# A two-layer decoder trunk on one Trainium2 core: a chained block pair makes its weight sum in place of a loaded tile, a fourth pair in the first FFN, and the mLSTM's output gate chained to its value pair

## The chip, the cores and the metric

The kernel runs on one core of one Trainium2 chip. The metric is the device time of one launch in microseconds (us). Before the change it is 1004.13 us, the median of 3 runs (1003.7 to 1004.54). A difference under 0.2%, about 2.0 us, can hardly be told from no change. The engines are named as the profile names them: PE is TensorE (matrix products), DVE is VectorE, ACT is ScalarE, POOL is GpSimd, SP is SyncE, which here only issues DMAs.

## The reference, cut to what matters

The input x is 256 tokens by 1024 features, f32. Two layers follow one another; each layer adds four sub-layers to x, and two of the four are FFNs:

```
def swiglu(x, w_in, w_out):
    gate, up = jnp.split(x @ w_in, 2, axis=-1)      # w_in 1024 x 5632
    return (jax.nn.silu(gate) * up) @ w_out         # w_out 2816 x 1024
...
h = swiglu(rms_norm(x, g[0]), w_ffn_in[layer, 0], w_ffn_out[layer, 0])
x = x + 0.5 * rms_norm(h, g[1])
h = rms_norm(x, g[2])
    # layer 0: mLSTM mixer, layer 1: differential attention
x = x + rms_norm(h, g[3])
h = swiglu(rms_norm(x, g[4]), w_ffn_in[layer, 1], w_ffn_out[layer, 1])
x = x + 0.5 * rms_norm(h, g[5])
gate = jax.nn.sigmoid(rms_norm(x, g[6]) @ w_ple_gate[layer])
x = x + rms_norm((p[layer] @ w_ple_proj[layer]) * gate, g[7])
```

The mLSTM mixer multiplies its input by one wide matrix, whose parts are the queries, keys, values (1024 columns) and the output gate o (1024 columns); its result is `(sigmoid(o) * h) @ w_out`. After layer 0 a shared K and V is made from x for the attention of layer 1. So there are four FFNs, called here FFN(0,0), FFN(0,1), FFN(1,0) and FFN(1,1) by layer and place.

## The kernel before, in words

**Tiles.** The 256 tokens are two tiles of 128 (t = 0 and 1). The 2816 hidden columns of an FFN are 11 blocks of 256 (`NJ`). A block's input weights are the 256 gate and the 256 up columns for 1024 features, 2 MB, which are loaded as two tiles of 1 MB, one for each half of the features. Such a tile is 128 partitions by 2048 f32 numbers and is called `wraw`. There are `NRAW` = 10 buffers of this kind; the attention and the mLSTM, the parameters of the norms and x itself lie in the same buffers.

**f32 products from three.** TensorE multiplies in a reduced f32 format here. So each operand is split in two parts, hi and lo, and a product is the sum of hi·hi, lo·hi and hi·lo (`mm3`, line 507). For a weight tile ACT writes the hi part (`whi`, 6 buffers, `NPART`) and DVE subtracts it from the tile for the lo part (`wlo`, 5 buffers, `NLOW`). A tile that is added or loaded therefore costs one pass of ACT and one of DVE over 2048 numbers. A product of a 128-token tile with half the features by one block is 12 matmuls of 128x512 (`times`).

**Pairs.** The function `block_pair` (line 718) takes two blocks of weights at a time. Two blocks, two token tiles and two feature halves are a 2x2 by 2x2 block product, and it is done with 7 products instead of 8, by sums of tokens (`forms`: s1, s2, s3, n4) and sums of weights. With b11 and b21 the two halves of the first block, b12 and b22 those of the second, the weight operands are: w11, w21 and w22 (tiles as loaded); t3 = b12 + b22 and u1 = b11 + b12 (made by a load and a second DMA on POOL's queue that adds into the loaded tile, an accumulate DMA); wt2 = b11 + t3 and wt4 = b21 + b11 (added by DVE). So a pair loads 5 tiles on SP's queue (b12 for t3, b11 for u1, b11, b21, b22) and accumulates 2 on POOL's. It keeps four products as copies that ACT takes out of the accumulator (`held`, rows `att<-accI`), and DVE adds or subtracts them. `PAIRS` (line 44) lists the first blocks of the pairs: 5, 7 and 9 in FFN(0,0), and 1, 3, 5, 7 and 9 in each other FFN. The blocks that are in no pair are done by 8 products a two of them. A pair that follows another one finds its t3 and u1 loaded already: the pair ahead of it issues these two loads with their accumulates (`nxt`, `ahead`). A pair of this kind is called chained here. The order of the products in a pair is w11, w21 (then `use(0, 0)`, the SwiGLU of block 0 and token tile 0), wt2, wu1, wt3, w22, wt4 (in the last pair of an FFN w22 stands ahead of wt3). Once a pair's seven products are recorded, the kernel records the output products of the blocks before it (`stage_out`, accumulators `accO`).

**mLSTM.** The value columns and the output-gate columns are two calls of `block_pair` (lines 1082 and 1170), each with all its own loads.

**The order of the work.** All operations are first recorded. A planner, `Notes.play` (line 290), then replays them on a model of the engines and queues: on each engine it takes, among what can start now, urgent work first and then the lowest rank, and it hands the buffers out in turn. `Notes.issue` (line 433) emits the result. So every instruction has line 433 in the profile, and groups are told apart by the names of the tiles. The names that matter: `wraw` a weight tile, `whi` and `wlo` its parts, `xh` and `xl` those of the tokens, `accI` the accumulators of the input products, `accO` those of the output products, `att` a held copy, `hh` and `hl` the parts of the hidden values, `sg` the SwiGLU.

The weight operands of a pair, in the order in which they are recorded before the change:

```
t3, u1 = ahead or (load(src2[0], src2[1]), load(src[0], src2[0]))
b11 = load(src[0])
w11 = parts(b11)
b21 = load(src[1])
w21 = parts(b21)
wt2 = add(b11, b11, t3)
wu1 = parts(u1)
wt3 = parts(t3)
b22 = load(src2[1])
w22 = parts(b22)
ahead = (load(nxt[1][0], nxt[1][1]), load(nxt[0][0], nxt[1][0])) if nxt else None
wt4 = add(b21, b21, b11)
```

## Time and profile before

| what | value |
|---|---|
| median of 3 runs | 1004.13 us (1003.7 to 1004.54) |
| the profiled execution: its own time | 1002.59 us |
| the profiled execution: its span | 1000.8 us |
| granted clock of TensorE, mean | 0.997 |
| PE busy | 986.4 us, 99% |
| DVE busy | 892.8 us, 89% |
| ACT busy | 698.6 us, 70% |
| moved by the DMA engines | 274.68 MB, mean 274 GB/s |

The span is the time from the first to the last record of the profile; 1.8 us of the execution's own time lie outside it. The profiled execution is 1.54 us quicker than the median. By the matmuls that read hidden values (`hh`), the FFNs lie in the span thus: FFN(0,0) from the start to about 190 us, FFN(0,1) from about 300 to 470, FFN(1,0) to about 720 (most of it from 575 on), FFN(1,1) from about 830 to about 970. Busy time of PE is from the start of a matmul to its modelled end, and matmuls overlap; a better measure of what a matmul costs is the distance between the starts of two in a row.

### The profile page before, as it was taken

The numbers are of one execution on the slowest core, as the hardware profiler recorded it, in microseconds if no ns is written. First come the engines' busy times: TensorE is split into PE (matmuls) and PEld (weight loads), VectorE is DVE, ScalarE is ACT, GpSimd is POOL, SyncE is SP. The second block draws the span as 40 slices with busy tenths as digits, with TensorE's granted clock in tenths as the row PEclk, the third lists the DMA queues.
The fourth block names the chain that finished last, engine by engine and source line by source line (L and its number), as shares of the span: only waits on it lengthen the run. The fifth ranks groups of instructions, "written<-read, shape, count | busy, mean of one in ns | idle before, by whom it ended". The sixth has DMA issues, their size and how long they took to land.

```text
span 1000.8 us, 12442 instructions
## 1 busy us (share of the span) xinstructions
PE 986.4 (99%) x4636; PEld 803.0 (80%) x4636; DVE 892.8 (89%) x909; ACT 698.6 (70%) x924; POOL 94.9 (9%) x126
## 2 busy tenths in 40 slices
PE   9999999999999999999999999999999999999997
PEld 7888888887787778888878888888888887878786
DVE  6977999799999999998799999898984999999983
ACT  7746777578756877685867767686776776757752
POOL 0010000300141000001120000001002300000010
PEclk9999999999999999999999999999999999999998
DMA  9999948765699999765699999864759899996621
GB/s 345 420 339 343 311 179 296 244 207 198 255 320 340 326 309 335 279 247 207 261 301 330 324 353 347 329 244 161 253 210 285 235 297 318 313 295 252 242 84 43
DMA packets 45859, 274.68 MB, mean 274 GB/s; under 512 B 5480, under 2 KB 5864, under 8 KB 16104
## 3 DMA queue, kind: packets, MB, share of 16 engines
q1 hardware_dynamic: 39752, 231.69, 60.2%
q0 software_dynamic: 5760, 41.95, 20.6%
q8 instruction: 36, 0.59, 0.2%
q10 hardware_dynamic: 288, 0.27, 0.1%
q14 instruction: 23, 0.19, 0.1%
HBM read 263.40 MB, written 10.49 MB: 274 GB/s over the span
## 4 chain that ended last, share of the span: by engine, by line
PE 47%; issue 2%; ACT 2%; POOL 1%; DVE 1%; DVEq 0%; POOLq 0%; ACTq 0%
PE accI L433 30%; PE accO L433 15%; PE tr L433 2%; POOL sm L433 1%; ACT sg L433 1%; DVE wlo_4r L433 0%; ACT att L433 0%; DVE wlo_2r L433 0%; ACT wraw L433 0%; ACT whi_5r L433 0%; ACT whi_0r L433 0%; DVE wraw L433 0%; DVE att L433 0%; DVE xl_5r L433 0%; DVEq L1498 0%
## 5 line engine op out<-in xcount | busy, mean ns | idle before, releaser
L433 DVE TENSOR_TENSOR wraw<-wraw,wraw 128x2048 f32<-128x2048 f32 x40 | 91.4, 2284 | 0.1
L433 ACT ACTIVATE whi_1r<-wraw 128x2048 fp32r<-128x2048 f32 (+2 forms) x49 | 72.7, 1494 | 18.2 <-PE accI L433 8.8
L433 ACT ACTIVATE whi_4r<-wraw 128x2048 fp32r<-128x2048 f32 (+1 forms) x45 | 75.4, 1684 | 11.9 <-issue 4.4
L433 ACT ACTIVATE whi_2r<-wraw 128x2048 fp32r<-128x2048 f32 (+1 forms) x48 | 79.4, 1661 | 5.5 <-issue 2.6
L433 ACT ACTIVATE whi_5r<-wraw 128x2048 fp32r<-128x2048 f32 (+1 forms) x47 | 79.2, 1694 | 5.6 <-PE accI L433 4.7
L433 ACT ACTIVATE whi_0r<-wraw 128x2048 fp32r<-128x2048 f32 (+2 forms) x48 | 74.5, 1557 | 6.8 <-PE accI L433 3.4
L433 ACT ACTIVATE whi_3r<-wraw 128x2048 fp32r<-128x2048 f32 (+1 forms) x45 | 73.6, 1647 | 3.3 <-PE accI L433 1.6
L433 ACT ACTIVATE att<-accI 128x512 f32<-128x512 f32 x80 | 47.5, 594 | 38.1 <-PE accI L433 37.8
L433 POOL DMA_DIRECT2D wraw<-in_ffn_in x36 | 32.0, 889 | 343.5 <-DMA wraw<-in_ffn_in 286.3
L433 POOL TENSOR_SCALAR sm<-sm 128x1 f32<-128x1 f32 x32 | 23.5, 735 | 308.8 <-ACT sg L433 308.8
L433 POOL TENSOR_TENSOR sm<-sm,mhalf 128x1 f32<-128x1 f32 (+2 forms) x40 | 30.7, 769 | 108.2 <-DVE sm L433 105.6
L433 ACT ACTIVATE sg<-att,sm 128x256 f32<-128x256 f32 x54 | 26.9, 502 | 16.9 <-DVE att L433 16.8
L433 ACT ACTIVATE sg<-accO 128x512 bf16<-128x512 f32 (+2 forms) x46 | 20.2, 445 | 25.0 <-PE accO L433 21.0
L433 ACT ACTIVATE sg<-accI,sm 128x256 f32<-128x256 f32 x34 | 16.0, 470 | 29.3 <-PE accI L433 27.3
L433 PEld LDWEIGHTS tr<-ident,sg 128*128 128x128 f32 x176 | 23.0, 140 | 14.6 <-DVE hl_2r L433 2.7
L433 PE MATMUL tr<-ident,sg 128*128 128x128 f32 x176 | 34.0, 274 | 0.3 <-DVE hl_2r L433 0.3
L433 DVE SCALAR_TENSOR_TENSOR wraw<-wraw,sm,wraw 128x512 f32<-128x512 f32 x32 | 22.7, 749 | 12.0 <-POOL sm L433 11.9
L433 DVE TENSOR_TENSOR att<-accI,att 128x512 f32<-128x512 f32 x40 | 27.4, 685 | 3.3 <-PE accI L433 2.9
L433 ACT ACTIVATE sg<-wraw 128x512 bf16<-128x512 f32 x32 | 20.1, 630 | 13.7 <-DVE wraw L433 9.7
L433 ACT ACTIVATE att<-accI,sm 128x512 f32<-128x512 f32 (+1 forms) x22 | 14.8, 671 | 20.8 <-PE accI L433 20.8
L433 DVE SCALAR_TENSOR_TENSOR sg<-att,sm,sg 128x256 f32<-128x256 f32 x54 | 25.7, 480 | 1.7 <-ACT sg L433 1.5
L433 DVE TENSOR_TENSOR att<-att,att 128x512 f32<-128x512 f32 (+1 forms) x33 | 22.4, 679 | 3.8 <-ACT att L433 3.6
(610 smaller groups left out, 3249.9 us busy)
## 6 DMA issues: line engine op xcount, KB each, us to landing
wraw<-in_ffn_in SPq DMA_DIRECT2D x102, 1024.0 KB, 9.4
wraw<-in_ffn_out SPq DMA_DIRECT2D x44, 1024.0 KB, 8.3
wraw<-in_ffn_in POOLq DMA_DIRECT2D x36, 1024.0 KB, 13.3
wraw<-in_mlstm_in SPq DMA_DIRECT2D x14, 1024.0 KB, 5.3
wraw<-in_ple_gate SPq DMA_DIRECT2D x8, 1024.0 KB, 5.1
wraw<-in_w_kv SPq DMA_DIRECT2D x8, 1024.0 KB, 4.8
home<-wraw SPq DMA_DIRECT2D x28, 256.0 KB, 5.1
wraw<-home SPq DMA_DIRECT2D x14, 512.0 KB, 5.4
```

What stands on the lines that cost most here:

```text
L433: getattr(getattr(self.nc, eng), name)(*args, **kw)
```

## The change

- `PAIRS`: FFN(0,0) has the pairs 3, 5, 7 and 9 (before: 5, 7 and 9). Blocks 3 and 4 were done by 8 products and are now done by 7.
- A chained pair has a new order of loads and products. Its second half-block b22 is loaded into a tile and split as w22; then b12 is accumulated onto the same tile by POOL's queue, so that it becomes t3. Before, t3 was a tile of its own, loaded by the pair ahead, and b22 a further load. The pair ahead now loads u1 alone. The order of the products is wu1, w22, w11, w21 (then `use(0, 0)`), then the output products of the pair ahead (`between`), then wt2, wt3 and wt4. Five products are held as copies instead of four.
- A pair that is the first of its chain keeps the order of before.
- The mLSTM's output gate is chained to its value pair: the value pair loads the gate's u1.
- `NRAW` goes from 10 to 9, `NLOW` from 5 to 6.

There are 3 chained pairs in FFN(0,0), 4 in each other FFN and 1 in the mLSTM, 16 in all. The numbers of instructions go from before to after as follows: 128x512 matmuls 4502 to 4490; loads of `in_ffn_in` tiles of 128x2048 on SP's queue 102 to 88, and of `in_mlstm_in` 14 to 13; accumulates on POOL's queue 40 to 42; DVE's splits of whole weight tiles 190 to 193, its adds of two weight tiles 40 to 42, its adds and subtracts of held copies and forms 72 to 75; ACT's copies out of `accI` into `att` 80 to 100.

The diff, cut to its core:

```
-NRAW = 10
+NRAW = 9
-NLOW = 5
+NLOW = 6
-PAIRS = ((5, 7, 9),) + ((1, 3, 5, 7, 9),) * 3
+PAIRS = ((3, 5, 7, 9),) + ((1, 3, 5, 7, 9),) * 3
...
+        if ahead is not None:
+            nc.is_urgent = False
+            u1 = ahead
+            t3 = load(src2[1])
+            nc.is_urgent = True
+            w22 = parts(t3)
+            nc.gpsimd.dma_start(t3, src2[0], accum_op=ALU.add)
+            nc.is_urgent = False
+            wu1 = parts(u1)
+            b11 = load(src[0])
+            w11 = parts(b11)
+            b21 = load(src[1])
+            w21 = parts(b21)
+            nc.is_urgent = True
+            s1, s2, s3, n4 = xf() if callable(xf) else xf
+            az = acc_in()
+            times(az, s1, wu1, False)
+            z5 = held(az)
+            times(az, n4, w22, True)
+            z4 = held(az)
+            ax, ay = acc_in(), acc_in()
+            times(ax, quarter(0, 0), w11, False)
+            p1 = held(ax)
+            times(ay, quarter(0, 4), w21, False)
+            nc.vector.tensor_tensor(p1, ay, p1, op=ALU.add)
+            use(0, 0, p1)
+            if between:
+                between()
+            nc.is_urgent = False
+            wt2 = add(b11, b11, t3)
+            ahead = load(nxt[0][0], nxt[1][0]) if nxt else None
+            wt3 = parts(t3)
+            wt4 = add(b21, b21, b11)
+            nc.is_urgent = True
+            times(ax, s2, wt2, True)
+            u2 = held(ax)
+            nc.vector.tensor_tensor(u2, z4, u2, op=ALU.subtract)
+            use(1, 0, u2)
+            times(ax, s3, wt3, True)
...
+            use(1, 1, z5)
+            times(ax, quarter(1, 4), wt4, True)
+            use(0, 1, ax)
+            return ahead
-        t3, u1 = ahead or (load(src2[0], src2[1]), load(src[0], src2[0]))
+        t3, u1 = load(src2[0], src2[1]), load(src[0], src2[0])
...
-        ahead = (load(nxt[1][0], nxt[1][1]), load(nxt[0][0], nxt[1][0])) if nxt else None
+        ahead = load(nxt[0][0], nxt[1][0]) if nxt else None
...
+            behind = [(i, t) for t in range(NT) for i in last]
             if len(item) == 2:
                 nxt = items[begin + n + 1]
+                between = late if split_begin and n == 0 else (lambda: outs(behind)) if ahead is not None else None
...
-        block_pair(xts, all_forms(), a["mlstm_in"][2], a["mlstm_in"][3], value)
+        gates = a["mlstm_in"][4:6]
+        ahead = block_pair(xts, all_forms(), a["mlstm_in"][2], a["mlstm_in"][3], value, nxt=gates)
...
-        block_pair(xts, all_forms(), a["mlstm_in"][4], a["mlstm_in"][5], opened)
+        block_pair(xts, all_forms(), *gates, opened, ahead=ahead)
```

What moves is shown at three places. The first is POOL's queue in FFN(0,0), where the accumulates stand with the semaphores that each waits for (`DMAHW` a load, `DVE` a split or add of VectorE). Before:

```order
L433 DMA wraw_83<-in_ffn_in 128x2048 [waits DMAHW7_49]
L433 DMA wraw_84<-in_ffn_in 128x2048 [waits DMAHW0_49]
L433 DMA wraw_79<-in_ffn_in 128x2048 [waits DMAHW5_49,DMAHW6_49,DMAHW4_49,DVE_49]
L433 DMA wraw_80<-in_ffn_in 128x2048 [waits DMAHW5_49]
L433 DMA wraw_84<-in_ffn_in 128x2048 [waits DMAHW3_49]
L433 DMA wraw_83<-in_ffn_in 128x2048 [waits DMAHW4_49]
```

After:

```order
L433 DMA wraw_79<-in_ffn_in 128x2048 [waits DMAHW3_49,DMAHW1_49,DMAHW4_49,DMAHW0_49,DVE_49]
L433 DMA wraw_80<-in_ffn_in 128x2048 [waits DMAHW5_49,DMAHW6_49,DMAHW1_49,DVE_49]
L433 DMA wraw_84<-in_ffn_in 128x2048 [waits DMAHW7_49]
L433 DMA wraw_78<-in_ffn_in 128x2048 [waits DMAHW1_49,DVE_49]
L433 DMA wraw_81<-in_ffn_in 128x2048 [waits DMAHW6_49]
L433 DMA wraw_85<-in_ffn_in 128x2048 [waits DMAHW7_49,DVE_49,Activation_49]
L433 DMA wraw_78<-in_ffn_in 128x2048 [waits DMAHW4_49]
L433 DMA wraw_81<-in_ffn_in 128x2048 [waits DMAHW0_49,DVE_49]
```

Two accumulates have come in ahead for the pair of blocks 3 and 4, and the accumulate of a chained pair's t3 (here `wraw_78`, the fourth) now waits for DVE, which splits the same tile as w22 first.

The second place is DVE at the start of FFN(1,1): the end of the attention's sum and the first pair's weights. `wlo` rows are splits, `wraw<-wraw,wraw` is a weight sum, and the last row is the residual add of token tile 1, from which the FFN's second token tile starts. Before:

```order
L433 TENSOR_TENSOR wlo_2r<-wraw_79,whi_4r 128x1024
L433 TENSOR_TENSOR wlo_3r<-wraw_76,whi_0r 128x1024 x2
L433 TENSOR_TENSOR wlo_1r<-wraw_78,whi_3r 128x2048
L433 TENSOR_TENSOR wraw_80<-accO_93,wraw_80 128x512
L433 TENSOR_TENSOR wraw_80<-accO_95,wraw_80 128x512
L433 TENSOR_TENSOR wlo_4r<-wraw_83,whi_5r 128x2048
L433 TENSOR_TENSOR wraw_78<-wraw_78,wraw_85 128x2048
L433 SCALAR_TENSOR_TENSOR sg_126<-accI_90,sm_6_162,sg_126 128x256
L433 SCALAR_TENSOR_TENSOR wraw_77<-wraw_80,sm_7_163,wraw_77 128x512 x2
```

After:

```order
L433 TENSOR_TENSOR wlo_3r<-wraw_82,whi_5r 128x1024
L433 TENSOR_TENSOR wlo_5r<-wraw_81,whi_0r 128x2048
L433 TENSOR_TENSOR wlo_1r<-wraw_85,whi_4r 128x2048
L433 TENSOR_TENSOR wraw_79<-accO_93,wraw_79 128x512
L433 TENSOR_TENSOR wraw_79<-accO_96,wraw_79 128x512
L433 TENSOR_TENSOR wraw_81<-wraw_81,wraw_83 128x2048
L433 TENSOR_TENSOR wraw_85<-wraw_85,wraw_81 128x2048
L433 SCALAR_TENSOR_TENSOR sg_128<-accI_92,sm_6_162,sg_128 128x256
L433 SCALAR_TENSOR_TENSOR wraw_84<-wraw_79,sm_7_163,wraw_84 128x512 x2
```

Both weight sums of the first pair now stand ahead of that residual add; before, only one did.

The third place is PE in FFN(1,1), where one accumulator goes from one product to the next. Before, the accumulator `accI_90` ends one product and starts the next four matmuls later:

```order
L433 MATMUL accI_90<-wlo_3r,xh_2r 128x512
L433 MATMUL accI_90<-whi_4r,xl_2r 128x512
L433 MATMUL accI_92<-whi_5r,xh_6r 128x512
L433 MATMUL accI_92<-wlo_1r,xh_6r 128x512
L433 MATMUL accI_92<-whi_5r,xl_6r 128x512
L433 MATMUL accI_92<-whi_5r,xh_6r 128x512
L433 MATMUL accI_90<-whi_3r,xh_3r 128x512
L433 MATMUL accI_90<-wlo_0r,xh_3r 128x512
```

After, `accI_91` does so, from wt2 to wt3 of a chained pair:

```order
L433 MATMUL accI_91<-wlo_3r,xh_0r 128x512
L433 MATMUL accI_91<-whi_1r,xl_0r 128x512
L433 MATMUL accI_90<-whi_2r,xh_2r 128x512
L433 MATMUL accI_90<-wlo_0r,xh_2r 128x512
L433 MATMUL accI_90<-whi_2r,xl_2r 128x512
L433 MATMUL accI_90<-whi_2r,xh_2r 128x512
L433 MATMUL accI_91<-whi_4r,xh_3r 128x512
L433 MATMUL accI_91<-wlo_1r,xh_3r 128x512
```

The four matmuls in between are of the next product; the number of such places with four matmuls in between goes from 7 to 20.

More of the change, by code (lines that the diff above doesn't have):

```diff
@@ L871, in late, with outs @@
             stage_out(0, 1)
+        def outs(todo, keep=0):
+            while len(todo) > keep:
+                stage_out(*todo.pop(0))
         def all_forms():
@@ L889, in ffn @@
                     stage_in(item[0], t)
-            for t in range(NT):
-                for i in last:
-                    stage_out(i, t)
+            outs(behind)
             last = item
@@ L908, in ffn @@
         else:
-            both(item, end=True, ahead=ahead)
-            for t in range(NT):
-                for i in last:
-                    stage_out(i, t)
+            behind = [(i, t) for t in range(NT) for i in last]
+            both(item, end=True, between=lambda: outs(behind, 1), ahead=ahead)
+            outs(behind)
             for t in range(NT):
```

41 lines of the change are left out of this document (21 added, 20 removed).

## The prediction, made before the changed kernel was run

> **What bounds the kernel now.** I read the page first, engine by engine and then the costliest groups.
>
> ```profile
> span 1000.8 us, 12442 instructions
> PE 986.4 (99%) x4636; PEld 803.0 (80%) x4636; DVE 892.8 (89%) x909; ACT 698.6 (70%) x924; POOL 94.9 (9%) x126
> L433 DVE TENSOR_TENSOR wraw<-wraw,wraw 128x2048 f32<-128x2048 f32 x40 | 91.4, 2284 | 0.1
> L433 ACT ACTIVATE att<-accI 128x512 f32<-128x512 f32 x80 | 47.5, 594 | 38.1 <-PE accI L433 37.8
> wraw<-in_ffn_in SPq DMA_DIRECT2D x102, 1024.0 KB, 9.4
> wraw<-in_ffn_in POOLq DMA_DIRECT2D x36, 1024.0 KB, 13.3
> ```
>
> PE is the bound: it idles only 14.4 of 1000.8 us. DVE follows at 89%. The last two rows are DMAs with their number and the median us from issue to landing: a load takes 9.4, an accumulate on POOL's queue 13.3. A share over the whole span hides what bounds a stage, so the next view is the busy time by stretches (columns: us, then busy us of PE, PEld, DVE, ACT, POOL; granted clock; DMA share; GB/s).
>
> ```profile
> 0.00:25.00 25.00, 23.23 (x97) 18.07 (x98) 16.29 (x35) 19.79 (x42) 2.48 (x11) 1.00 0.93 344
> 25.00:125.00 100.00, 100.00 (x453) 82.38 (x452) 86.64 (x73) 65.08 (x63) 5.39 (x6) 1.00 1.02 353
> 250.00:375.00 125.00, 122.78 (x563) 97.92 (x562) 120.79 (x128) 89.16 (x116) 20.30 (x18) 1.00 0.94 309
> 575.00:800.00 225.00, 224.95 (x1138) 184.65 (x1137) 195.51 (x226) 159.34 (x266) 24.23 (x32) 1.00 0.78 269
> 800.00:850.00 50.00, 47.67 (x212) 38.05 (x211) 49.23 (x44) 37.05 (x39) 3.56 (x4) 1.00 0.94 307
> 975.00:1001.00 26.00, 18.35 (x104) 16.00 (x102) 8.99 (x15) 7.49 (x16) 2.02 (x5) 0.90 0.12 45
> ```
>
> So the idle time has places: 1.8 us at the start, 2.2 around the start of FFN(0,1) (250 to 375 us), 2.3 around that of FFN(1,1) (800 to 850), 7.65 in the tail behind the last product. The change touches neither start nor tail. At the two FFN starts DVE is the full engine (120.8 of 125, 49.2 of 50 us). In the second FFN(0,0) stretch, 25 to 125 us, the DMA engines are saturated, share 1.02, and still PE is busy throughout: no load is waited for there.
>
> **What the change removes on PE.** One product of 12 matmuls goes (blocks 3 and 4 by 7 instead of 8). The chain of waits has the pace of a long run of matmuls:
>
> ```profile
> 593.25 15.90 PE accI L433 x70
> ```
>
> 15.90 / 70 = 0.227 us each, 12 × 0.227 = **−2.7**. As PE is busy all through 25 to 125 us, it comes off the end, if DVE keeps up. The Trainium skill, TensorE: Matmul & The Clock Gate, section Back-to-back issue gap, gives about 131 ns a matmul at N = 512 as a sustained roofline (216 ns for the isolated gap); by 131 the product would be worth an estimated 1.57 us and the sum below would be −2.5; the trace's 227 ns decides.
>
> **The starts of FFN(0,1) and FFN(1,1).** Here is DVE at the second one, with the PE rows that wait.
>
> ```profile
> 826.95 2.28 DVE L433 TENSOR_TENSOR wraw<-wraw,wraw 128x2048 f32<-128x2048 f32 x1
> 829.14 0.42 DVE L433 TENSOR_TENSOR hl_1r<-tr,hh_1r 128x256 fp32r<-128x256 f32 x1
> 830.43 2.28 DVE L433 TENSOR_TENSOR wlo_2r<-wraw,whi_5r 128x2048 fp32r<-128x2048 f32 x1
> 832.63 0.48 DVE L433 SCALAR_TENSOR_TENSOR sg<-att,sm,sg 128x256 f32<-128x256 f32 x1
> ```
>
> ```profile
> 831.23 0.50 PE L433 MATMUL accI<-whi_0r,xh_2r 128*128 128x512 f32 x1 [1.06 <-ACT whi_0r L433]
> 832.76 0.50 PE L433 MATMUL accI<-wlo_2r,xh_5r 128*128 128x512 f32 x1 [1.03 <-DVE wlo_2r L433]
> ```
>
> PE waits for a split that DVE starts only after a 2.2-us weight sum (829.14 − 826.95). In the changed order the first pair's second sum stands ahead of the last residual add (the DVE rows above), so DVE comes in one 2.2-us pass ahead. Behind that, a chained pair starts with wu1, w22, w11 and w21, which need splits only, then the output products of the pair ahead, four in all, 4 × 2.7 = 10.9 us of PE for two DVE splits; its sums wt2 and wt4 are needed only then. Before, the sum wt2 was wanted as third product. The two starts idle 2.2 + 2.3 = 4.5 us. The ends are 0 (what was stalled is stalled elsewhere) and −4.5. A lead of 2.2 at each covers most of both, but one of the two waits at 831 us is ACT's, which a lead on DVE need not end; I take two thirds, **−3.0**.
>
> **Accumulators that turn around.** With the new order wt2 and wt3 of a chained pair use one accumulator in a row: ACT must copy it out before PE writes it again, and only a few matmuls lie between. The trace shows both kinds of case, two matmuls between and four.
>
> ```profile
> 838.09 0.39 PE L433 MATMUL accI<-whi_4r,xh_6r 128*128 128x512 f32 x1
> 838.31 0.39 PE L433 MATMUL accO<-whi_3r,hh_2r 128*128 128x512 f32 x1
> 838.93 0.50 PE L433 MATMUL accI<-whi_1r,xh_3r 128*128 128x512 f32 x1 [0.23 <-ACT att L433]
> ...
> 870.50 0.39 PE L433 MATMUL accI<-whi_5r,xh_6r 128*128 128x512 f32 x1
> 870.73 0.44 PE L433 MATMUL accI<-whi_3r,xh_3r 128*128 128x512 f32 x1
> 871.01 0.39 PE L433 MATMUL accI<-wlo_0r,xh_3r 128*128 128x512 f32 x1
> ```
>
> With four the next start is 871.01 − 870.73 = 0.28 instead of 0.23: 0.05 lost. With two the gap is 838.93 − 838.31 = 0.62 instead of 0.23: 0.39 lost. In the changed order 13 more places have four between (7 to 20): 13 × 0.05 = 0.65. Two places with two between become three with one, three and one; each matmul missing of four costs a further 0.2, so about 0.4 × 2 before and 0.6 + 0.25 + 0.6 now, +0.65. Sum **+1.3**; the ends are 0 and, were each of the 13 as dear as one with two between, 13 × 0.39 = +5.
>
> **The new pair in FFN(0,0).** Its t3 is loaded and accumulated early, in the saturated stretch. The two rows are the SP loads there (one of them lands 15.8 us after its issue) and POOL's first accumulates of before.
>
> ```profile
> 18.40 1.59 SPq L433 DMA_DIRECT2D wraw<-in_ffn_in  x2
> wraw<-in_ffn_in SPq DMA_DIRECT2D x1, 1024.0 KB, 15.8
> 49.45 1.06 POOL L433 DMA_DIRECT2D wraw<-in_ffn_in  x1 [28.63 <-DMA wraw<-in_ffn_in]
> wraw<-in_ffn_in POOLq DMA_DIRECT2D x1, 1024.0 KB, 12.9
> 52.27 0.39 PE L433 MATMUL accI<-whi_2r,xh_0r 128*128 128x512 f32 x1
> ```
>
> If t3's load lands where that load did, 18.4 + 15.8 = 34.2, the accumulate is in at 34.2 + 1.06 (POOL's issue) + 12.9 = 48.2. DVE then owes a sum and three splits, 4 × 2.2 + 0.34 = 9.1, so wt2 is ready at about 57.3. PE is at the pair's first product at 52.27, at wt2 two products later, 52.27 + 2 × 2.7 = 57.7. The margin is 0.4 us, and one landing 3 us later eats it. Beyond that the pair adds 12.8 us to DVE between 25 and 125 us: three splits and two sums of 2.2 and three small adds of 843.57 − 842.97 = 0.6, by these rows:
>
> ```profile
> 842.97 0.69 DVE L433 TENSOR_TENSOR att<-att,att 128x512 f32<-128x512 f32 x1
> 843.57 1.22 DVE L433 TENSOR_TENSOR wlo_2r<-wraw,whi_3r 128x1024 fp32r<-128x1024 f32 x1
> ```
>
> And DVE had 100 − 86.6 = 13.4 free there. It just fits; I take **+0.7**, ends 0 and +3.
>
> **What costs nothing, and by what cover.** Fifteen loads of 1 MB go and two accumulates come: −13 MB of 274.68. Where the share is over 1 PE waits for no load, so 0 here; it speeds other landings, which is the cover for R2 below. One end is −1 (the waits at starts), the other 0. Twenty more copies out of accumulators are 20 × 0.594 = 11.9 us of ACT, at 70%; their cover is ACT's idle time, and the copies on the path are the turnarounds above. The tenth buffer goes, but each chained pair needs one tile fewer; the attention and the mLSTM hold theirs: 0, end +3 if a load of the next stage has to wait for one. The sixth `wlo` lets DVE run ahead by one more split, which is in the lead above. The mLSTM's gate pair: between its w22 split and its wt2 sum DVE has 19.3 us of other work, more than an accumulate takes: 0.
>
> **The sum.** −2.7 − 3.0 + 1.3 + 0.7 = −3.7; the profiled execution's 1002.59 becomes 998.9, and as it lay 1.54 below the median, the median 1004.13 becomes **1000.5**.
>
> **The rivals.** *R1: stalls change place.* DVE's load grows by 12.8 us and its order is as full as before at the two starts, so nothing is won there: −2.7 + 1.3 + 0.7 = −0.7, or 1003.4. For it: DVE is 97 to 98% busy in both stretches. Against it: the lead is in the order, and the splits come ahead of the sums.
>
> *R2: slower, by the in-order chain split, accumulate, sum.* A chained t3 can be accumulated only when DVE has split it as w22, and DVE's in-order queue stands at the sum wt2 until it has landed; all later splits wait behind that, then PE. Before, t3 was loaded a pair ahead. By the changed order, DVE's work between the two, at 2.2 a whole pass, is 16.3, 21.0, 19.2 us in FFN(0,0), 19.3 in the mLSTM, 18.6, 24.0, 18.8, 21.8 in FFN(0,1), 14.5, 18.8, 21.8, 21.8 in FFN(1,0), 18.9, 24.0, 18.8, 21.8 in FFN(1,1). What an accumulate takes in this trace:
>
> ```profile
> DMA to landing us min/median/max: 8.7/13.3/19.0
> ...
> 782.05 0.93 POOL L433 DMA_DIRECT2D wraw<-in_ffn_in  x1 [1.41 <-DVE xl_0r L433]
> 794.46 0.94 POOL L433 DMA_DIRECT2D wraw<-in_ffn_in  x1
> wraw<-in_ffn_in POOLq DMA_DIRECT2D x2, 1024.0 KB, 9.0
> ```
>
> At the median with a us for the issue none of the 16 waits. At the longest, 19, and 2 more for semaphores and issue, 21 in all, they would wait 4.7 + 1.8 + 1.7 + 2.4 + 2.2 + 6.5 + 2.2 + 2.1 + 2.2 = some 26; at 17 and 2, 2.7 + 0.4 + 4.5 and four of 0.1 to 0.2, some 8.3, which I price as the likelier of the two. By that, −3.7 + 8.3 = +4.6, or **1008.7**. It decides from a landing of about 13.5 us (the tightest pair, FFN(1,0)), and in earnest from 17. For it: half of the accumulates take over 13.3. Against it: before, most were issued in twos, t3's with u1's; the two that went alone, at 782 and 794 us, took 9.0, and t3's now goes alone, with fewer loads beside it. The Trainium skill, DMA: Bandwidth & Descriptors, section Anatomy of one DMA (SWDGE, gpsimd), has 2.0 us and bytes over 436 GB/s, an estimate of 4.4 us for 1 MiB; by it R2 could never come. The trace's shortest is 8.7, twice that, so the margins above stand.
>
> *R3: all stalls of the starts go and the turnarounds are hidden*: −2.7 − 4.5 = −7.2, or 996.9. For it: DVE's lead and fewer bytes in the stretches where the share is 0.94. Against it: the 0.05 and 0.39 stand in the trace.
>
> *R4: the edits don't do what they say on the clock:* a saved load where no load was waited for brings nothing; that is in the sum already, so it has no chance of its own.
>
> **How the numbers follow.** The forecast 0.54, R1 0.20, R2 0.14, R3 0.12. A measurement of this kernel tells about 0.2%, 2.0 us, from no change: 1002.1 to 1006.1 is the same. The forecast's own range is 998 to 1002.5, by the ends of two terms that weigh most: −1.5 more at the starts with −1 for the transfers, or 2 more at the new pair; a tenth of it falls in same. R3 and nine tenths of the forecast are faster, 0.12 + 0.5 = 0.62 and a little of R1: 0.65. R1 and the rest are same, 0.22; R2 makes slower, 0.13. The range takes in R3 and R1, and the +5 of dear turnarounds; it leaves out R2 from half its price on: 996.0 to 1006.0.
>
> **What would show it.** In the changed profile: PE's idle at 250 to 375 and 800 to 850 us down from 4.5 to about 1.5; in the list of PE's waits, `att` up by about 1.3; DVE with no idle of over 1 us ahead of a `wraw<-wraw,wraw` row released by a DMA (otherwise R2); accumulates still at 9 to 15 us; PE busy without a gap at 50 to 70 us, and FFN(0,0) 2 us shorter. It is wrong if PE idles in FFN(0,0) at the pair of blocks 3 and 4, if DVE waits for accumulates, or if a new wait for a load shows at the attention or the mLSTM, where the tenth buffer was.

## The result, and the profile of the changed kernel

| | before | changed |
|---|---|---|
| median | 1003.01 us (20 runs, 1001.78 to 1004.54) | 1005.61 us (20 runs, 1003.01 to 1007.34) |
| profiled execution: own time, span, granted clock | 1002.59, 1000.8, 0.997 | 1005.54, 1003.8, 0.995 |

The ratio is 1.0025, with a 95% interval from 1.0019 to 1.0032: slower by about 2.6 us, where 3.6 us faster was forecast. One of the eleven launches of the kernel fill_three below took 2565.92 us and is left out of its figures. The page of the changed kernel first, with the lines that answer to those of before:

```profile
span 1003.8 us, 12378 instructions
PE 988.7 (99%) x4624; PEld 804.3 (80%) x4624; DVE 905.4 (90%) x917; ACT 709.4 (71%) x947; POOL 90.4 (9%) x128
L433 ACT ACTIVATE att<-accI 128x512 f32<-128x512 f32 x100 | 58.7, 595 | 78.2 <-PE accI L433 77.5
L433 DVE TENSOR_TENSOR wraw<-wraw,wraw 128x2048 f32<-128x2048 f32 x42 | 96.0, 2285 | 0.4
```

PE has twelve matmuls fewer and is busy 2.3 us longer. So they run slower somewhere. DVE's 12.6 us more and ACT's 10.8 us more are near what was counted, 12.8 and 11.9. The stretches, in the same columns as before:

```profile
25.00:125.00 100.00, 98.88 (x443) 80.25 (x442) 94.46 (x76) 69.76 (x72) 6.26 (x7) 1.00 1.00 339
125.00:250.00 125.00, 123.60 (x577) 99.72 (x576) 115.64 (x115) 88.64 (x102) 9.21 (x17) 0.99 0.72 228
250.00:375.00 125.00, 122.25 (x562) 98.98 (x561) 116.52 (x130) 90.14 (x120) 19.34 (x17) 0.99 0.88 281
800.00:850.00 50.00, 50.00 (x231) 40.76 (x231) 48.26 (x48) 39.50 (x47) 4.89 (x6) 1.00 0.82 267
```

The start of FFN(1,1), 800 to 850 us, has no idle time left (2.3 us before). FFN(0,0) has 1.1 us of it that was not there, the mLSTM 1.4 us by 250 us, and the start of FFN(0,1) 2.7 us. And in two stretches the granted clock is 0.99 where it was 1.00. Cut finer, the same view shows what that is:

```profile
225.00:227.50 2.50, 2.10 (x11) 1.50 (x10) 2.43 (x6) 2.50 (x2) 0.89 (x1) 0.81 0.50 52
227.50:230.00 2.50, 2.50 (x7) 1.95 (x7) 2.50 (x6) 2.47 (x4) 0.00 (x0) 0.50 0.84 167
...
302.50:305.00 2.50, 0.47 (x5) 0.47 (x5) 1.74 (x3) 2.47 (x4) 2.04 (x3) 1.00 0.00 0
305.00:307.50 2.50, 2.50 (x12) 2.08 (x10) 2.13 (x5) 1.67 (x6) 0.85 (x2) 0.51 0.82 121
307.50:310.00 2.50, 2.50 (x11) 2.06 (x10) 2.39 (x5) 2.50 (x5) 0.00 (x0) 0.80 1.04 234
```

The clock falls to one half, for 3.4 us, and each time that costs 1.7 us: 2.5 × 0.49 + 2.5 × 0.20 = 1.7 at 305 us, 2.5 × 0.19 + 2.5 × 0.50 = 1.7 at 225 us. PE's timeline shows what lies ahead of the two falls, and what matmuls cost in them. At the end of the mLSTM:

```profile
301.91 0.39 PE L433 MATMUL accI<-whi_4r,xl_3r 128*128 128x512 f32 x1
304.53 0.66 PE L433 MATMUL tr<-ident,wraw 128*128 128x128 f32 x4 [2.23 <-DVE wraw L433]
304.95 0.67 PE L433 MATMUL accI<-whi_4r,xh_3r 128*128 128x512 f32 x1
...
306.12 0.78 PE L433 MATMUL accI<-wlo_4r,xh_3r 128*128 128x512 f32 x1
306.69 0.63 PE L433 MATMUL accI<-whi_4r,xl_3r 128*128 128x512 f32 x1
```

And in the mLSTM:

```profile
222.13 1.47 PE L433 MATMUL accO<-wraw 128*128 128x256 f32 x8
224.61 0.50 PE L433 MATMUL accI<-whi_4r,xh_3r 128*128 128x512 f32 x1 [1.01 <-ACT xh_3r L433]
...
227.13 0.80 PE L433 MATMUL accI<-whi_4r,xl_3r 128*128 128x512 f32 x1 [0.25 <-DVE xl_3r L433]
227.72 0.63 PE L433 MATMUL accI<-whi_4r,xh_3r 128*128 128x512 f32 x1
228.15 0.63 PE L433 MATMUL accI<-wlo_4r,xh_3r 128*128 128x512 f32 x1
```

Behind each stall matmuls start 0.43 us (228.15 − 227.72) and more apart, instead of 0.23. The first stall, 2.23 us, is PE's wait for the residual add of token tile 1; the second, 1.26 us in two parts, stands among small matmuls. The kernel before has no such fall between its start and its tail.

Set out by stage, PE's waits in us are (from its timeline, summed), with the falls of the clock beside them:

| us of the span | 0–25 | 25–195 | 195–300 | 300–350 | 350–700 | 700–800 | 800–850 | 850– | falls |
|---|---|---|---|---|---|---|---|---|---|
| before | 1.7 | 0 | 0.4 | 1.1 | 0.8 | 0 | 2.3 | 0.3 | none |
| changed | 1.9 | 1.1 | 1.3 | 2.7 | 0.3 | 0.5 | 0 | 0 | 2 × 1.7 |

Each row is one execution, and waits differ between executions of the same work: in the first 25 us the run layer1 below, whose order is there that of the kernel before, has 2.5 us against 1.7. So of the 3.0 us by which the span grew: −2.7 for the product, +1.1 for waits (7.8 against 6.7), +3.4 for the clock. The 1.2 us that are left lie in delays too short to be listed as waits: outside waits and falls, the mean distance of two 128x512 matmuls that follow one another goes from 232.3 to 232.7 ns, 0.4 ns on some 3730 of them, 1.5 us; the tail behind the last product is 0.4 us shorter.

### The profile page after: what moved, and what is told of

Its sections match the earlier page's. It is cut to its first block, busy times and chain, and to the rows that moved or that the text cites. A ratio compares the mean times of both kernels' runs of the same rounds, so it can differ in the third digit from the quotient of the medians.

```text
span 1003.8 us, 12378 instructions
## 1 busy us (share of the span) xinstructions
PE 988.7 (99%) x4624; PEld 804.3 (80%) x4624; DVE 905.4 (90%) x917; ACT 709.4 (71%) x947; POOL 90.4 (9%) x128
## 5 line engine op out<-in xcount | busy, mean ns | idle before, releaser
L433 ACT ACTIVATE whi_1r<-wraw 128x2048 fp32r<-128x2048 f32 (+2 forms) x52 | 78.5, 1517 | 12.6 <-PE accO L433 7.8
L433 DVE TENSOR_TENSOR wlo_0r<-wraw,whi_0r 128x2048 fp32r<-128x2048 f32 (+2 forms) x26 | 48.6, 1874 | 3.0 <-ACT whi_0r L433 3.0
L433 DVE TENSOR_TENSOR wlo_0r<-wraw,whi_2r 128x2048 fp32r<-128x2048 f32 (+1 forms) x25 | 48.5, 1943 | 1.8 <-ACT whi_2r L433 1.8
L433 DVE TENSOR_TENSOR wlo_1r<-wraw,whi_4r 128x2048 fp32r<-128x2048 f32 (+1 forms) x23 | 46.1, 2006 | 2.5 <-ACT whi_4r L433 2.5
L433 DVE TENSOR_TENSOR wlo_2r<-wraw,whi_3r 128x2048 fp32r<-128x2048 f32 (+1 forms) x23 | 44.0, 1914 | 3.9 <-ACT whi_3r L433 3.8
L433 DVE TENSOR_TENSOR wlo_3r<-wraw,whi_3r 128x2048 fp32r<-128x2048 f32 (+1 forms) x23 | 46.1, 2004 | 0.7 <-ACT whi_3r L433 0.7
L433 DVE TENSOR_TENSOR wlo_1r<-wraw,whi_1r 128x2048 fp32r<-128x2048 f32 (+2 forms) x28 | 46.7, 1672 | 0.0
L433 DVE TENSOR_TENSOR wlo_5r<-wraw,whi_0r 128x2048 fp32r<-128x2048 f32 (+1 forms) x23 | 43.7, 1912 | 0.0
L433 DVE TENSOR_TENSOR wlo_5r<-wraw,whi_5r 128x2048 fp32r<-128x2048 f32 (+1 forms) x21 | 43.6, 2081 | 0.1
L433 DVE TENSOR_TENSOR wlo_4r<-wraw,whi_1r 128x2048 fp32r<-128x2048 f32 (+1 forms) x20 | 37.0, 1856 | 0.3 <-ACT whi_1r L433 0.3
L433 DVE TENSOR_TENSOR wlo_2r<-wraw,whi_2r 128x2048 fp32r<-128x2048 f32 (+1 forms) x18 | 34.6, 1928 | 0.3 <-ACT whi_2r L433 0.2
```

The costliest lines, as they stand in the source:

```text
L433: getattr(getattr(self.nc, eng), name)(*args, **kw)
```

## The experiments

The theory that I took from this (A): the loss is made in two stalls, in the mLSTM and at its end, and over half of it is the fall of the clock that a stall sets off. Rivals: moving work only moves the waits (B), the chained gate pair costs (C), the fourth pair costs (D), and later: the buffers (F) or the order of the products (G) put DVE's passes where they stand. Each group of rows was timed beside the kernel before on one chip; "clock" is the mean of the granted clocks over a kernel's executions.

| kernel | median us | before, beside it | ratio and interval | clock |
|---|---|---|---|---|
| late_sum | 1008.77 | 1002.30 (clock 0.9981) | 1.0064 (1.0052 to 1.0076) | 0.9938 |
| fill | 1005.03 | | 1.0028 (1.0019 to 1.0037) | 0.9961 |
| gate_alone | 1005.90 | | 1.0038 (1.0024 to 1.0052) | 0.9965 |
| before_four | 1008.57 | | 1.0061 (1.0049 to 1.0073) | 0.9964 |
| after_again | 1005.61 | 1002.87 (0.9974) | 1.0026 (1.0016 to 1.0036) | 0.9962 |
| fill_two | 1003.56 | | 1.0009 (1.0000 to 1.0017) | 0.9978 |
| idle_before | 1005.14 | | 1.0020 (1.0011 to 1.0029) | 0.9968 |
| three_pairs | 1004.78 | | 1.0016 (1.0005 to 1.0027) | 0.9968 |
| late_split | 1007.12 | 1004.01 (0.9973) | 1.0041 (1.0028 to 1.0054) | 0.9957 |
| both_moved | 1007.08 | | 1.0042 (1.0026 to 1.0058) | 0.9950 |
| both_three | 1010.42 | | 1.0068 (1.0055 to 1.0080) | 0.9920 |
| before_n9 | 1011.72 | 1003.51 (0.9975) | 1.0088 (1.0075 to 1.0101) | 0.9950 |
| layer1 | 1005.19 | | 1.0022 (1.0013 to 1.0031) | 0.9980 |
| after_n10 | 1011.77 | | 1.0087 (1.0069 to 1.0105) | 0.9960 |
| fill_again | 1005.12 | 1003.47 (0.9975) | 1.0016 (1.0007 to 1.0025) | 0.9966 |
| fill_three | 1003.67 | | 1.0006 (0.9997 to 1.0015) | 0.9981 |

### Is it the clock? Filler in the stalls

The edit, in words of code: ahead of the first transpose at 302 us (and, in fill_two, ahead of the product at 224 us) matmuls are issued whose results the transposes overwrite.

```
+    if i == at:
+        for _ in range(9):
+            self.nc.tensor.matmul(pt, self.last[1], self.last[2], start=True, stop=True)
```

The run "fill", the stall at 302 us alone:

> The changed kernel with nine idle-time matmuls of 128x512 (about 2.05 us) into the transposes' bank right ahead of the transposes that PE waits for at 302 us; their results are overwritten. Everything else stands in the same order. Theory A says that the wait itself stays (PE is busy with filler for most of 2.2 us), but the granted clock no longer falls to 0.5 behind it: matmuls at 305 to 308 us at 0.23 instead of 0.43 to 0.57 us, 1.5 to 2 us less than the changed kernel, about 1003.8. Rival B (the slow matmuls at 305 us have another cause than the idle time): no change, 1005 to 1006.

Its profiled execution shows no fall of the clock and no slow matmuls, at 305 us or elsewhere. But its median is 1005.03, rival B's number, with a ratio of 1.0028, the same as the changed kernel's 1.0025 within the intervals, and the mean clock of its executions, 0.9961, is no higher than the changed kernel's (0.9956, and 0.9962 in the next group). Filler at 302 us alone gained nothing that can be seen; the other stall was still there. Next comes the changed kernel itself, timed beside the runs that follow:

> The changed kernel again, beside the other three on the same chip, as their yardstick: 2 to 3 us above the kernel before, as measured first. Theory A has its times in steps of about 1.7 us, by how many stretches of 3.4 us at half the granted clock an execution has: the mean granted clock of an execution and its time go together, 1 us for 0.001.

1005.61 and 1.0026, as at first. Over the first 20 executions of the changed kernel the clock and the time go together: four with a clock of 0.997 or more have a mean of 1003.96 us, eight with 0.995 or less one of 1006.41. The slope is 0.7 to 0.8 us for 0.001, not 1. One reason may be the idle tail, where the clock falls too and costs nothing (4.1 to 7.5 us long in the 18 profiles). The slope alone proves little: the kernel before, whose profile has no fall ahead of its tail, has one of 0.55 to 0.77 in the five groups. And the steps of 1.7 us that I expected are not there: the times of the changed kernel lie at 1003.0 to 1003.2, 1004.1 to 1004.3, 1005.5 to 1005.7 and without a gap from 1006.1 to 1007.3.

> The changed kernel with filler matmuls in both stalls: nine of 128x512 ahead of the transposes at 302 us and four ahead of the product at 224 us, in the mLSTM. All else in the same order. Theory A (half of the loss and more is the fall of the granted clock behind these two stalls): the clock of its executions rises to that of the kernel before (0.998), and the time falls by 2 to 3 us to 0 to 1 us above the kernel before. Rival B (the fall of the clock is by chance or has other causes): clock and time as the changed kernel's, 2 to 3 us above.

1003.56, 2.05 us less than the changed kernel beside it (1.7 by the ratios), ratio 1.0009, and the clock is up from 0.9962 to 0.9978, that of the kernel before or above. This is the run on which theory A rests. In its profile the filler stands where the wait was, and the matmuls behind it keep their pace (0.23 us, where they took 0.43 and more):

```profile
301.25 1.98 PE L1559 MATMUL tr<-whi_4r,xl_3r 128*128 128x512 f32 x8
303.06 0.60 PE L433 MATMUL tr<-ident,wraw 128*128 128x128 f32 x4
...
305.46 0.40 PE L433 MATMUL accI<-whi_0r,xl_5r 128*128 128x512 f32 x1
305.70 0.40 PE L433 MATMUL accI<-whi_0r,xh_5r 128*128 128x512 f32 x1
```

The same kernel, timed again, came out at 1.0016, with a clock of 0.9966 and one fall left, at 227.5 us, in the profiled execution:

> The changed kernel with the filler matmuls in both stalls once more, as yardstick for the next run: 0 to 1.5 us above the kernel before, clock at 0.998.

1005.12 lies 1.65 above the kernel before, a little over the range. So filler takes 1 to 2 us off (the lower figure with intervals that overlap). In the mLSTM PE runs the same instructions at the same distances in both profiles of this kernel, and ahead of 227.5 us its only listed wait is 0.34 us; the clock fell in one and not in the other.

The opposite edit puts a stall into the kernel before, two DVE passes ahead of the residual:

```
+    if i == at:
+        for _ in range(2):
+            self.nc.vector.tensor_tensor(hg, hg, hg, op=ALU.max)
```

> The kernel before with one thing added: two DVE passes of 128x1024 (2.26 us, the larger of a tile and itself, so nothing changes in the values) right ahead of the residual add at 298.85 us, the place where the changed kernel has one pass more. Theory A: PE waits 2 us longer at 300 us, and in most executions the clock then falls for 3.4 us: 3 to 4 us slower than the kernel before. Rival B (the pass alone counts): 2.0 to 2.3 us slower. Rival E (PE has other work or makes it good later): within 1 us.

1005.14, 2.3 us slower, ratio 1.0020 (1.0011 to 1.0029): rival B's number, not A's. The profile at the place of the edit:

```profile
301.19 0.66 PE L433 MATMUL tr<-ident,wraw 128*128 128x128 f32 x4 [1.78 <-DVE wraw L433]
301.60 0.48 PE L433 MATMUL accI<-whi_5r,xl_5r 128*128 128x512 f32 x1
301.91 0.60 PE L433 MATMUL accI<-ident,wraw 128*128 128x128 f32 x4
302.27 0.48 PE L433 MATMUL accI<-whi_5r,xh_5r 128*128 128x512 f32 x1
```

The wait came out at 1.78 us, not over 2, and no fall follows (0.31 us apart, with transposes between). A fall of 3.4 us does stand in this profile, at 835.4 us, behind the wait of 2.1 us at the start of FFN(1,1), which the kernel before has too, without a fall behind it. So this run does not give the price of a wait alone. I then counted, in all 18 profiles, PE's waits of at least 0.9 us (summed within 3.4 us; the first 25 us, where no fall stands, left out) and whether the clock fell behind them. From 2.2 to 3.6 us it fell in 8 of 9; at 2.0 to 2.1 us in 2 of 6; from 1.0 to 1.8 us in none of 10. In the mLSTM at 225 us, where the matmuls around the wait are small, 1.0 to 1.4 us were enough in 4 of 7. The Trainium skill, TensorE: Matmul & The Clock Gate, Part 1, has a free-running window of about 3.4 us after which an idle array runs at half its clock; the halves and the 3.4 us agree with these rows, and so does that the same wait may or may not set it off. Where the clock stays down longer, it is for two or three times 3.41 us: 6.8 in late_sum and both_three, 10.2 in after_n10. The rule in the same page of the Trainium skill, section HAM oscillation — how this bites in real kernels, no idle gaps of more than about 3.4 us, is too wide here: 2.2 us were enough, and one wait of 3.55 us in late_split was not.

### Can the stalls be moved away? Three orders

In late_sum the sum that stands ahead of the residual goes behind it; the split (below) stays.

```
 TENSOR_TENSOR wraw_81<-accO_96,wraw_81 128x512
-TENSOR_TENSOR wraw_80<-wraw_80,wraw_84 128x2048
 TENSOR_TENSOR wlo_0r<-wraw_83,whi_0r 128x2048
 SCALAR_TENSOR_TENSOR wraw_85<-wraw_81,sm_2_158,wraw_85 128x512 x2
```

> The changed kernel with one thing moved: the first pair's sum b21... of FFN(0,1) (DVE's whole pass wraw<-wraw,wraw that starts at 298.48 us in the changed profile) and ACT's copy of it stand behind the residual add of token tile 1 and the forms that follow, instead of ahead of it. PE's order is the same. Theory A (the loss is made at the mLSTM's end: one more DVE pass ahead of the residual, 2.2 us of PE idle at 302 us, and then 3.5 us at half the granted clock): the wait at 302 us goes, the clock stays at 1.00 there, 3 to 4 us less than the changed kernel, so 1001.6 to 1002.6. Rival B (the pass is only put off, DVE is full and PE waits behind it instead): within 1 us of the changed kernel, 1004.6 to 1006.6.

1008.77: 3 to 4 us slower than the changed kernel (1.0064 against 1.0025), worse than either theory had it. DVE waits for ACT's copy of the next tile, which the sum had covered, so the residual comes 5.5 us behind the adds instead of 6.45, not 2.2 us sooner. PE's wait at 302 us is down to 0.47 us, but the sum that was put off delays the SwiGLU behind it. In this profile the clock falls for 6.8 us at 228 us and for 3.4 us behind the new wait, and the mean clock is 0.9938. Two rows, DVE's and PE's:

```profile
301.26 2.29 DVE L433 TENSOR_TENSOR wlo_0r<-wraw,whi_0r 128x2048 fp32r<-128x2048 f32 x1 [2.02 <-ACT whi_0r L433]
```

```profile
319.59 0.44 PE L433 MATMUL tr<-ident,sg 128*128 128x128 f32 x2 [2.97 <-DVE sg L433]
```

In late_split the split wlo_0r goes behind the residual instead. In both_moved, besides, ACT's copy and DVE's split of the token form xh_3r, xl_3r go ahead of a weight pass in the mLSTM.

> The changed kernel with one DVE instruction moved: the split (wlo_0r, 2.2 us) that stands right ahead of the residual add of token tile 1 at the mLSTM's end stands right behind it, with one small operation between. All other engines in the same order. Theory A (the pass ahead of the residual makes the wait at 302 us, and the wait lets the clock fall): the wait of 1.4 to 2.2 us there goes, about 0.9 us of a new wait for that split comes, and the clock stays up there: 1.5 to 2.5 us less than the changed kernel, so 0 to 1.2 us above the kernel before. Rival B (DVE is full, and the wait comes back in full length behind, as it did when the sum was moved): within 1 us of the changed kernel, or slower.

> As the run with the late split, and in the mLSTM ACT's copy and DVE's split of the token form that PE waits for at 224 us each stand one weight pass earlier. Theory A: the stall of 1.0 and 0.3 us at 224 us goes and the clock no longer falls there, another 1.3 to 2.5 us: 2.5 to 4.5 us less than the changed kernel, so 1001 to 1003, 0 to 2 us below the kernel before. Rival B: no more than the 1.3 us of the wait, and given back behind it.

1007.12 and 1007.08, both about 1.5 us slower than the changed kernel by their ratios (1.0041 and 1.0042 against 1.0026): rival B. The residual came in time, and PE then stood still for the forms that DVE had not got to, in late_split

```profile
306.24 0.41 PE L433 MATMUL tr<-ident,sg 128*128 128x128 f32 x2 [3.55 <-DVE att L433]
```

and in both_moved both there and in the mLSTM, where the gates' scan came too late:

```profile
226.46 1.12 PE L433 MATMUL accO<-sg,ident 4*128 4x256 f32 x4 [2.01 <-DVE sg L433]
```

In all three orders, what was moved ahead in DVE's queue made something else late.

### What are the parts worth?

The gate pair by itself, as two lines undone:

```
-        ahead = block_pair(xts, all_forms(), ..., value, nxt=gates)
+        block_pair(xts, all_forms(), ..., value)
-        block_pair(xts, all_forms(), *gates, opened, ahead=ahead)
+        block_pair(xts, all_forms(), *gates, opened)
```

> The changed kernel with the mLSTM's output gate as a pair of its own again, all five tiles loaded, old order of products; FFNs as in the changed kernel. Theory A: DVE has the same two passes ahead of the residual at the mLSTM's end (a sum and a split), so the wait at 300 us and the fall of the clock stay, and the stall at 224 us lies ahead of the gate pair: within 1 us of the changed kernel, 1004.6 to 1006.6. Rival C (the chained gate pair costs: its accumulate and the five held copies stand in the mLSTM's way): 2 to 4 us less, 1001.6 to 1003.6.

1005.90, 1.0038: undoing the chain gains nothing, where rival C had 2 to 4 us. But the stalls that I expected to stay are not there: neither that at 302 us (0.7 us in all from 300 to 350 us) nor that at 225 us, which I had put ahead of the gate pair. A larger one, of 3.2 us in two parts, with a fall of the clock, is at 267 us, as in before_n9 below. So with nine and six buffers the chained gate brings two stalls and takes one away; what it costs by itself this run does not show.

The fourth pair, in the order of before and left out of the changed kernel:

```
-PAIRS = ((5, 7, 9),) + ...      before_four, in the kernel before
+PAIRS = ((3, 5, 7, 9),) + ...
-PAIRS = ((3, 5, 7, 9),) + ...   three_pairs and fill_three, in the changed kernel
+PAIRS = ((5, 7, 9),) + ...
```

> The kernel before with the fourth pair in FFN(0,0) alone (blocks 3 and 4 by 7 products, t3 and u1 of each chained pair loaded as before, ten wraw and five wlo buffers, mLSTM as before). Theory A: the product that goes is worth its 2.7 us less the 0.5 to 1.5 us of waits that a fuller DVE makes, and the order at the mLSTM's end is that of before (two splits behind the adds), so 1000.3 to 1002.0. Rival D (DVE is full in FFN(0,0), with 12.8 us more to do in 100 us, and waits eat the product): 1002.5 to 1004.

1008.57, 6.3 us slower: beyond rival D. In the order of before the fourth pair makes PE wait 4.6 us in FFN(0,0), with a fall of the clock:

```profile
84.12 0.49 PE L433 MATMUL accI<-whi_5r,xh_6r 128*128 128x512 f32 x1 [1.49 <-ACT att L433]
85.41 0.80 PE L433 MATMUL accI<-wlo_1r,xh_2r 128*128 128x512 f32 x1 [0.80 <-DVE wlo_1r L433]
86.01 0.63 PE L433 MATMUL accI<-whi_0r,xl_2r 128*128 128x512 f32 x1
86.43 0.63 PE L433 MATMUL accI<-whi_0r,xh_2r 128*128 128x512 f32 x1
```

That makes 4.6 + 1.7 − 2.7 = 3.6 us; where the rest of the 6.3 arises I did not trace.

> The changed kernel with the pairs of FFN(0,0) as before, 5, 7 and 9; in-place sums, buffers and the mLSTM as changed. Theory A (the fourth pair is worth its product less about a us of waits; the loss is in the mLSTM and at its end): 1 to 2 us slower than the changed kernel, 3.5 to 4.5 us above the kernel before. Rival D (the fourth pair costs time also in the new order, as it does in the old one): 2 to 4 us faster than the changed kernel, 0 to 1 us off the kernel before.

1004.78, 0.8 us faster than the changed kernel beside it, between the two expectations and with intervals that overlap. Two more runs, meant to be without the stalls:

> As the run before this one, but with the pairs of FFN(0,0) as before the change, 5, 7 and 9; both moves are made at the same places. With the two stalls out of the way, this shows what the fourth pair is worth. Theory A (2.7 us of product less 1.8 us of waits in FFN(0,0) by the profiles): 0.5 to 1.5 us slower than with four pairs. Rival D (the fourth pair costs as much as it saves, or more): 0 to 1.5 us faster than with four pairs.

1010.42 against 1007.08: three pairs 3.3 us slower, but its clock is 0.9920, and in its profile the clock falls for 6.8 us at 227 us and again at 308.5. The moved orders had made the stalls longer, so this comparison says nothing of the pair.

> The same filler in the changed kernel with three pairs in FFN(0,0), so that the fall of the clock blurs neither and the difference of the two is what the fourth pair is worth. By the waits that PE has between 25 and 195 us, 1.1 us with four pairs and none with three, the fourth pair's 2.7 us of product should leave 1 to 1.6 us: theory A has three pairs slower by 0.7 to 2 us. Rival D (the pair costs as much as it saves, in delays too short to be listed as waits): within 0.5 us, or three pairs faster.

1003.67 against 1005.12 of fill_again, 1.45 us faster with three pairs (1.0 by the ratios), again with intervals that overlap (1.0006, 0.9997 to 1.0015, against 1.0016, 1.0007 to 1.0025) and with a clock of 0.9981 against 0.9966, which by the slope above is 1.1 us. In the profiles FFN(0,0)'s last output matmul starts at 183.62 us with four pairs and at 184.06 with three: the product's 2.7 us leave 0.4. PE waits 1.1 us more there (0.5 for a SwiGLU of DVE, 0.6 for ACT's copy of a weight tile); the other 1.2 lie in delays too short to be listed. Apart from both_three, no run shows a gain from the pair, as rival D had it.

### Buffers or order?

The kernel before with the buffers of the changed one, the changed one with those of before, and the new order in the second layer only:

```
-NRAW = 10            before_n9; after_n10 has these lines the other way
+NRAW = 9
-NLOW = 5
+NLOW = 6
...
+        if ahead is not None and place:          layer1, with place=l == 1
```

> The kernel before with the buffers of the changed one alone: nine wraw and six wlo. In its order DVE has, at the mLSTM's end, 13.7 us of work between the residual adds of the two token tiles (before 11.5, changed 13.7), with a sum and a split ahead of the second, and both sums at the end of the attention, as the changed kernel. Theory F (the buffers, not the new order, put DVE's passes ahead): the wait at 302 us of 1.4 to 2.6 us with the clock's fall, and no wait at 831 us, and elsewhere as before: 1 us faster to 2 us slower than the kernel before. Rival G (the in-place order does it): waits as before, the 2.1 us at 831 us among them, within 1 us of the kernel before.

1011.72, 8.2 us slower than the kernel before. F is right on the start of FFN(1,1): with these buffers its 2.3 us of PE idle are gone, in the order of before. It is wrong on the place and the size of the loss. Of 800 to 850 us before_n9 has

```profile
800.00:850.00 50.00, 49.77 (x228) 39.76 (x226) 48.53 (x47) 41.86 (x48) 5.85 (x6) 1.00 0.93 287
```

and in the mLSTM the same stall as gate_alone, where the kernel before has 0.4 us of waits:

```profile
268.08 0.66 PE L433 MATMUL tr<-ident,wraw 128*128 128x128 f32 x4 [1.08 <-DVE wraw L433]
270.88 0.50 PE L433 MATMUL accI<-wlo_0r,xh_4r 128*128 128x512 f32 x1 [2.15 <-DVE wlo_0r L433]
...
272.57 0.63 PE L433 MATMUL accI<-wlo_0r,xh_4r 128*128 128x512 f32 x1
```

Its profiled execution is its quickest (1008.06), so a part of the 8.2 us is not in this profile.

> The new order for the chained pairs of FFN(1,0) and FFN(1,1) alone, with ten wraw and five wlo; layer 0 in the order of before, three pairs in FFN(0,0), the gate pair alone. Up to FFN(1,0) it is instruction for instruction the kernel before. Theory F (the gain at FFN(1,1) is the sixth wlo's): the 2.1 us of wait at 831 us stay, the accumulators' turnarounds add about 1: 0 to 2 us slower than the kernel before. Rival G (the new order's splits-first start is what keeps PE fed there): the wait goes, 1.5 to 3 us faster than the kernel before.

1005.19, 1.7 us slower, as F had it, and with a clock of 0.9980, as high as that of the kernel before: this loss is no fall of the clock. The new order alone gains nothing at FFN(1,1). With five `wlo` it has one wait less at the start and one later. In all its waits add up to 8.5 us against 6.7, as much more as it lost, though 0.9 us of that stands ahead of 350 us, where its order is that of before:

```profile
824.79 0.50 PE L433 MATMUL accI<-wlo_2r,xh_6r 128*128 128x512 f32 x1 [1.17 <-DVE wlo_2r L433]
```

```profile
883.66 0.50 PE L433 MATMUL accI<-wlo_2r,xh_5r 128*128 128x512 f32 x1 [1.31 <-DVE wlo_2r L433]
```

> The changed kernel with the buffers of before, ten wraw and five wlo. DVE has 16.4 us of work between the two residual adds at the mLSTM's end. Theory F: the wait at 302 us is no shorter than in the changed kernel, the wait at 831 us is there again: 1 to 4 us slower than the changed kernel, 3.5 to 7 us above the kernel before. Rival G: within 1 us of the changed kernel.

1011.77, 6 us slower than the changed kernel by its ratio, again F's sign, a little beyond its range in the ratio to the kernel before (8.3 us). But F's reason fails at 302 us: the wait that it had as no shorter is gone, and that at 831 us is 1.2 us. PE's waits are 12.6 us in all, and in the mLSTM the clock falls for 10.2 us in the profiled execution, 5.1 us of loss. So each kernel is poor with the other's buffers; which of the two numbers does it was not tested.

## Why the prediction was wrong

The median, 1005.61, lies inside the stated 996.0 to 1006.0, but that range was wide; the way was wrong. Of the signs that I named, PE's idle time in the two stretches is 2.75 us and not 1.5, FFN(0,0) is 0.6 us shorter and not 2, and the waits for `att` went down.

**The product, −2.7.** Twelve matmuls went, and the step is right as far as PE's own work. What it leaves is 0.4 us at the end of FFN(0,0). The term for the new pair, +0.7 with ends 0 and +3, was mis-sized: 2.7 − 0.4 = 2.3, near the end that I did not take. DVE did keep up with the t3 that I had timed; PE waited for a SwiGLU and for a copy of ACT instead (1.1 us). Its side sum with 1.57 us for the product comes to −2.6, not −2.5.

**The starts, −3.0.** This is the step that failed, and with it the two terms that I put at 0 for the tenth buffer and the gate pair. At FFN(1,1) it is right in size (2.3 us of idle time went) and half wrong in its reason: the buffers alone do it in the order of before (before_n9), the order that starts with splits does not (layer1). At FFN(0,1) it has the wrong sign: PE's waits there went from 1.1 to 2.7 us. I read the weight sum ahead of the residual add as a lead of one DVE pass. But the residual add is itself what PE waits for. The timelines of DVE up to that add, of the kernel before

```profile
292.40 1.29 DVE L433 TENSOR_TENSOR wraw<-accO,wraw 128x512 f32<-128x512 f32 x2 [0.21 <-PE accO L433]
293.60 2.28 DVE L433 TENSOR_TENSOR wlo_2r<-wraw,whi_5r 128x2048 fp32r<-128x2048 f32 x1
295.80 2.28 DVE L433 TENSOR_TENSOR wlo_4r<-wraw,whi_2r 128x2048 fp32r<-128x2048 f32 x1
298.85 1.42 DVE L433 SCALAR_TENSOR_TENSOR wraw<-wraw,sm,wraw 128x512 f32<-128x512 f32 x2 [0.77 <-POOL sm L433]
```

and of the changed one

```profile
293.87 0.69 DVE L433 TENSOR_TENSOR xl_3r<-att,xh_3r 128x512 fp32r<-128x512 f32 x1 [1.78 <-ACT xh_3r L433]
294.48 0.69 DVE L433 TENSOR_TENSOR xl_5r<-att,xh_5r 128x512 fp32r<-128x512 f32 x1
295.08 2.28 DVE L433 TENSOR_TENSOR wlo_4r<-wraw,whi_4r 128x2048 fp32r<-128x2048 f32 x1
297.28 1.28 DVE L433 TENSOR_TENSOR wraw<-accO,wraw 128x512 f32<-128x512 f32 x2
298.48 2.28 DVE L433 TENSOR_TENSOR wraw<-wraw,wraw 128x2048 f32<-128x2048 f32 x1
300.68 2.29 DVE L433 TENSOR_TENSOR wlo_0r<-wraw,whi_0r 128x2048 fp32r<-128x2048 f32 x1
303.73 1.41 DVE L433 SCALAR_TENSOR_TENSOR wraw<-wraw,sm,wraw 128x512 f32<-128x512 f32 x2 [0.76 <-POOL sm L433]
```

show two things. From the adds to the residual both kernels take 6.45 us, with two passes between; the changed one has one pass more ahead of the adds (the split wlo_4r, 2.2 us). And ahead of that split DVE stands still for 1.78 us, for a token form that ACT makes late, since ACT's queue stands at a weight tile that has not landed:

```profile
291.41 1.92 ACT L433 ACTIVATE whi_4r<-wraw 128x2048 fp32r<-128x2048 f32 x1 [1.97 <-DMA wraw<-in_ffn_in]
293.23 0.61 ACT L433 ACTIVATE xh_3r<-att 128x512 fp32r<-128x512 f32 x1
```

The load that lands just ahead of this copy was issued at 279.07 us, after SP had waited 7.3 us for DVE's split wlo_3r, by which, as far as the profile tells, a tile came free; it took 12.2 us. The length of PE's wait follows this idle time of DVE: 2.23 us with 1.78 here, 1.43 with 0.97 in after_again, 2.58 with 2.13 in three_pairs, each time some 0.45 more. So the pass used up the slack, and by these profiles the late load made most of the wait. That is the case for which I gave the tenth buffer an end of +3, and one of my signs of being wrong, a new wait for a load at the mLSTM. With ten and five buffers (after_n10), or with the gate not chained (gate_alone, before_n9), ACT waits for no load there and PE for 0.2 us at most. No run moves that load alone. R1, that stalls change place, is what happened at this start, with a price that it lacked.

**What the sum lacked: the clock.** Every row of the prediction but the tail's (0.90) had a granted clock of 1.00, so I counted a wait at its own length. Two of the new waits were each followed by 3.4 us at half the clock, +3.4 in the profiled execution. By the clocks of the runs (0.9956 over the 20 changed ones, 0.9974 to 0.9981 for the kernel before) and the slope above it is 1.3 to 2.0 us in the mean; fill_two gives 2.05 back, and fill_again, at 1.65 above the kernel before, some 1.0 of the 2.6. So by these estimates it is between two fifths and four fifths of the loss; fill, with filler at 302 us alone, showed none of it.

**The mLSTM, 0.** Wrong by 0.9 us of waits and by one of the two falls. I had timed the gate pair's accumulate and not what its weights displace. ACT copies a weight tile (1.9 us, at 220.53 us) ahead of the token form xh_3r, which in the kernel before came first, and PE waits 1.0 us for it. This wait is in all seven profiles with the chained gate that have neither filler nor a moved form there, with nine or ten buffers, and in none of the six with the gate as a pair of its own. Without the chain the nine and six buffers make another stall (before_n9 and gate_alone, 3.2 us at 267 us). I did not settle which of the two numbers, nine or six, does it.

**Turnarounds, +1.3.** Over-priced. In the distances of consecutive matmuls the sum of delays between 0.03 and 0.08 us goes from 1.0 to 1.3, +0.3, and the waits for copies from 0.7 to 0.45.

**R2, 8.3 us, with 0.14.** It did not come. DVE waits for one DMA alone, at its start, in the changed kernel, and the accumulates became quicker (8.7, 13.3 and 19.0 before):

```profile
DMA to landing us min/median/max: 7.9/11.3/17.6
```

That 15 loads went gained nothing that these runs show, as forecast; a load did come late, at 291 us. R3's saving needed all stalls to go; fill_two, with PE's waits at 4.7 us and no fall of the clock in its profile, still is not below the kernel before.

What stays open: how much of the 2.6 us the falls make, since the two runs of the same filler kernel differ by 1.6 us; how much the late load makes; and which of the two buffer numbers matters where. No version here beats the kernel before.
